# Paddings between the ring of weights and the blocks of h in place of one strip, in a decoder layer of attention and gated linear attention

## The chip, the cores and the metric

The kernel runs on one core of a Trainium2 chip. The metric is the device time of one execution in microseconds (us). Three runs of the kernel before gave a median of 979.86 us (979.69 to 980.12).

## The reference, cut to what matters

One layer for 1024 tokens of width 1024, in float32:

```python
h = rms_norm(x, pre_g)
z = einsum('bsd,de->bse', h, w_in)          # w_in: 1024 x 7184
qa, ka, va, ga, qb, kb, vb, gb, gk_low = split_columns(z)
oa = diff_attention(qa, ka, va, lam)        # 8 heads, two softmax maps each
ob = gla_chunked(qb, kb, vb, log_a)         # 4 heads, from gk_low
y = einsum('bse,ed->bsd', concatenate([oa * silu(ga), ob * silu(gb)]), w_out)
return x + rms_norm(y, post_g)
```

(The norms of `oa` and `ob` are left out here.) The part that the change touches is the first product, `h @ w_in`.

## The kernel before

**Arithmetic.** TensorE multiplies in the type `float32r`, which keeps fewer digits than float32. So each operand is split into a `hi` and a `lo` tile, and a product is three matmuls: hi by hi, lo by hi and hi by lo.

**Stage 1, `h @ w_in`, to about 625 us.** h transposed is cut into four blocks of 512 by 512, and the weights likewise; a pair of column groups (list `pairs`) is computed by seven block products in place of eight (numbers 1 to 7; dictionary `LEFT`, line 319, says which block of h or which sum of blocks each takes: h11, h12, h22, s1 to s4). The list `order` holds all products in the order in which they are done; `go` (line 595) steps through it, prepares the weights of the present and the next three products (`prepare`, `make_weights`), and calls `step`, which calls `multiply` (line 322). A *narrow* product is 12 matmuls: the weights (128 by 128) are the stationary operand and a 512-column row block of h is the moving one. A *wide* product (the values, VA and VB) is 24 matmuls with the roles exchanged: 128 columns of h are stationary and 256 columns of the weights are moving. Results x, y and z stay in banks of PSUM, are copied out by ScalarE (`snap`, line 427) and added by VectorE (line 440).

**Weights.** SyncE loads raw weights to `w_raw`. VectorE forms sums of blocks there (line 296), ScalarE rounds to the hi tile (line 315), VectorE subtracts to the lo tile (line 316). Hi and lo go to the **ring**: five tiles of 4096 bytes in each partition (`tag="ring"`, `bufs=NRING`). A narrow product takes one ring tile for both, a wide pair takes two. Each of the ring's 196 tiles replaces an earlier one: where several are waited for, the pool takes the one that is released first (28 times the tile taken was handed out four before, and 28 times six before; else five).

**Blocks of h.** Each block has hi and lo, each in two pieces of 4096 bytes (s3 and s4 in one piece of 8192). They lie in the pools `hw` and `hpool` at the right end of SBUF. Ahead of `hw` the kernel allocates a strip `edge` of 120 float32 (480 bytes in a partition) at the very end (lines 124 and 125), which nothing reads. When h is no longer needed, the same places of `hw` hold `wo_hi`, `wo_lo` (the weights w_out) and `m_hi`, `m_lo` (the concatenated heads).

**Stage 2, attention and output.** From about 275 us parts of the gated linear attention (`gla`, whose norm is the two matmuls `gms` with the constant `ones` as stationary operand, lines 839 to 841) are strewn into stage 1; `low_rank` (matmuls `gkl_ps`, with `wl2` stationary, 64 columns) and `decay` (`gk`) run early. From about 625 us `merge` interleaves the attention's scores (`sc`), transposes (`wtr`), weighted values (`po`) and the first part of the output product (`ypart`); the rest of that (`yps`) ends the kernel.

**Order.** All matmuls and transposes go through the helpers `mm` (line 117) and `tr` (line 120), which pin them in the program's order, so nearly all TensorE work has line 117. The other engines' instructions are ordered by the recording layer's planner.

**Offsets.** What follows calls the byte address of an operand in its partition, modulo 512, its *offset*. In the program before, all five ring tiles, all blocks of h, `wo`, `m`, q, k, v and the transposed attention weights have offset 0, and since matmul operands begin at multiples of 128 elements in them, so has nearly every matmul operand. The exceptions: `ident` (the moving operand of the transposes) is at 160, `ones` at 192, and `wl2`, whose slices of 64 columns lie alternately at 0 and 256. While one matmul streams its moving operand, the stationary operand of the next is loaded; the *distance* of such a pair is the offset of the operand that is loaded minus that of the one that is streamed, modulo 512.

Of the kernel before, what the change touches and what calls it, by code (L numbers as in the profile page):

```python
# [8 lines left out]
F32 = mybir.dt.float32  # L9
F32R = mybir.dt.float32r  # L10
# [4 lines left out]
P = 128  # L15
# [4 lines left out]
HB = 4  # L20
# [11 lines left out]
def hymba_kernel(  # L32
# [21 lines left out]
    act, dve, pool, pe, sp = nc.scalar, nc.vector, nc.gpsimd, nc.tensor, nc.sync  # L54

    def fp(t):
        return t.bitcast(F32)
# [63 lines left out]

    edge = ctx.enter_context(tc.tile_pool(name="edge", bufs=1, side="right"))
    pool.memset(edge.tile([P, 120], F32, name="edge"), 0.0)
    hw = ctx.enter_context(tc.tile_pool(name="hw", bufs=1, side="right", reuse_waits="tile"))
    hpool_cm = tc.tile_pool(name="hpool", bufs=1, side="right")
    hpool = hpool_cm.__enter__()

    H = {}  # L130

    def block(n):
        if n not in H:
            pool_h, pieces = (hpool, 1) if n in ("s3", "s4") else (hw, 2)
            H[n] = [
                [
                    pool_h.tile(
                        [P, HB // pieces, 512], F32R, tag=f"{n}_{part}{i}", name=f"{n}_{part}"
                    )
                    for i in range(pieces)  # L140
                ]
                for part in ("hi", "lo")
            ]
        return H[n]
# [5 lines left out]
    for n in ("h11", "h12"):  # L150
        block(n)
# [3 lines left out]
    ap = ap_cm.__enter__()  # L155
# [25 lines left out]
    def wide(p):  # L181
        return pairs[p][0] in ("VA", "VB")
# [3 lines left out]
    def load_raw(p, halves=(0, 1)):  # L186
        if p >= len(pairs):
            return
        c0 = pairs[p][2]
        for kh in halves:  # L190
            if kh not in raws.setdefault(p, {}):
                r = ap.tile([P, HB, 256], F32, tag="raw", name="w_raw", bufs=4)
                rows = slice(kh * 512, kh * 512 + 512)
                sp.dma_start(r, w_in[0, rows, c0 : c0 + 256].rearrange("(k p) c -> p k c", p=P))
                raws[p][kh] = r
# [21 lines left out]
    i = order.index((1, 4))  # L217
# [20 lines left out]
    def prepare(i):  # L238

        if i >= len(order) or i in ws:  # L240
            return
        if i < 4:

            act_ins, dve_ins = normed[0][:2]
            with tc.issue_after(act_ins.ins), tc.issue_after(dve_ins.ins):
                make_weights(i)
        else:
            make_weights(i)

    def fetch_raw(p, n, i):  # L250

        if not wide(p):
            load_raw(p)
            if i >= n_early:
                load_raw(p + 1)
        elif p >= 4 or p == 0:
            load_raw(p)
            if p and n == 1:
                load_raw(p + 1)

            if n == 4:
                load_raw(p + 2, (0,))
                if p == 0:
                    load_raw(3, (0,))
            elif n == 7:
                if p == 0:
                    load_raw(3, (1,))
                else:
                    load_raw(p + 2, (1,))
        else:  # L270
            if n == 5:
                load_raw(2, (1,))
            elif n == 4:
                load_raw(4, (0,))
            elif n == 7:
                load_raw(4, (1,))

    def make_weights(i):
        p, n = order[i]
        if wide(p) and p % 2:  # L280
            ws[i] = ws_wide[p - 1, n]
            return
        if p in early and n < 3:
            src = early[p][n - 1]
        else:
            fetch_raw(p, n, i)
            if wide(p):
                (b11, b21), (b12, b22) = ([raws[q].get(kh) for kh in range(2)] for q in (p, p + 1))
            else:
                top, bot = raws[p][0], raws[p][1]  # L290
                b11, b12 = top[:, :, :P], top[:, :, P:]
                b21, b22 = bot[:, :, :P], bot[:, :, P:]


            def sub(dst, a, b):
                dve.tensor_tensor(dst, a, b, ALU.subtract)  # L296
                return dst

            if n == 5:
                src = sub(b11, b12, b11)  # L300
            elif n == 6:
                src = sub(b11, b22, b11)
            elif n == 4:
                src = sub(b21, b21, b11)
            elif n == 7:
                src = sub(b12, b22, b12)
            else:
                src = {1: b11, 2: b21, 3: b22}[n]
        if wide(p):
            w = [ap.tile([P, HB, 256], F32R, tag="ring", name="w", bufs=NRING) for _ in range(2)]  # L310
            ws_wide[p, n] = w
        else:
            w2 = ap.tile([P, 2, HB, P], F32R, tag="ring", name="w", bufs=NRING)
            w = [w2[:, 0], w2[:, 1]]
        act.copy(w[0], src)  # L315
        dve.tensor_tensor(w[1], src, fp(w[0]), ALU.subtract)  # L316
        ws[i] = w

    LEFT = {1: "h11", 2: "h12", 3: "s4", 4: "h22", 5: "s1", 6: "s2", 7: "s3"}
    NRING = 5  # L320
# [224 lines left out]
    def parts(n, j, f):  # L545
        hi, lo = block(n)
        act.copy(at(hi, j), f)
        dve.tensor_tensor(at(lo, j), f, fp(at(hi, j)), ALU.subtract)  # L548

    def blocks(j):  # L550


        pss = []
        for k in (j, j + HB):
            ps, i = take_bank([P, 512], "xT")
            for n in range(4):
                tr(ps[:, n * P : (n + 1) * P], xs[4 + n][:, k * P : (k + 1) * P])
            pss.append(ps)
            free.append(i)
        k = j + HB  # L560
        h21 = t_c("h21")
        act.activation(h21, pss[0], AF.Copy, scale=pre_g[:, j : j + 1])
        put(pss[1], k, block("h22"), j)
        s1 = t_c("s1")
        dve.scalar_tensor_tensor(s1, pss[1], pre_g[:, k : k + 1], h21, ALU.mult, ALU.add)
        parts("s1", j, s1)
        h11 = f1[0][:, j]
        dve.tensor_tensor(h21, h11, h21, ALU.subtract)
        dve.tensor_tensor(h11, s1, h11, ALU.subtract)
        parts("s2", j, h11)  # L570
        parts("s3", j, h21)
# [436 lines left out]
    w, used, scored, opened = {}, set(), [], {}  # L1008
# [517 lines left out]
```

## Time and profile before

| | |
|---|---|
| median of 3 runs | 979.86 us |
| profiled execution | 979.08 us, of which the profile's span is 977.4 us |
| granted TensorE clock, mean | 0.999 |
| VectorE, ScalarE, GpSimd busy | 735.4, 600.5, 142.9 us |
| moved by DMA | 220.45 MB, mean 226 GB/s |

How to read it: the page has the busy time of each engine (PE is TensorE's matmuls, PEld its weight loads, DVE VectorE, ACT ScalarE, POOL GpSimd), then the span in 40 slices, then the chain of work that ended last. A matmul's recorded duration covers its way through the array and overlaps with the next one's. So the rate of TensorE is read from the *starts*: in the timeline a row has the start of a run of equal matmuls and ends in their count (x8), and the next row's start less this one's, divided by the count, is the time per matmul.

### The profile page before, as it was taken

The page shows a single profiled execution, that of the slowest core. Times are in us where ns is not written, and L with a number is a line of the kernel's source. Part 1 is how long each engine was busy: PE and PEld are TensorE (multiplying, and loading weights), DVE is VectorE, ACT ScalarE, POOL GpSimd, SP SyncE. Part 2 cuts the span into 40 slices and gives each one's busy share as a digit, 9 for nine tenths or more (in the row PEclk, how much of TensorE's full clock was granted, in tenths as well). Part 3 has the DMA queues.
Part 4 walks back from the last instruction along what each step waited for, and adds up shares of the span by engine and source line. Part 5 has one row for each costly group of instructions (what it writes and reads, how often), then busy time and mean ns, then how long its engine had stood idle before and what let it go on. Part 6 is the DMA issues. An engine that isn't in the chain of part 4 may idle for free.

```text
span 977.4 us, 15766 instructions
## 1 busy us (share of the span) xinstructions
PE 956.7 (98%) x5338; PEld 830.4 (85%) x5338; DVE 735.4 (75%) x1452; ACT 600.5 (61%) x1164; POOL 142.9 (15%) x158
## 2 busy tenths in 40 slices
PE   5999999999999999999999999999999999999997
PEld 5998988888889998999888888878888888888785
DVE  6887597789866667686786876487888888898554
ACT  8742455487357455454665775366776687887773
POOL 4300000000000010000200002121322222443321
PEclk9999999999999999999999999999999999999999
DMA  9432446656774868897987866987656669994677
GB/s 345 151 110 91 139 135 205 231 179 225 238 247 162 264 187 286 254 294 229 293 259 243 273 202 191 407 269 272 197 186 228 240 199 344 340 294 105 151 208 147
DMA packets 152593, 220.45 MB, mean 226 GB/s; under 512 B 17104, under 2 KB 83664, under 8 KB 152416
## 3 DMA queue, kind: packets, MB, share of 16 engines
q1 hardware_dynamic: 146176, 203.71, 64.1%
q0 software_dynamic: 6336, 15.73, 7.0%
q8 instruction: 42, 0.69, 0.3%
q14 instruction: 39, 0.32, 0.1%
HBM read 133.93 MB, written 88.60 MB: 228 GB/s over the span
## 4 chain that ended last, share of the span: by engine, by line
PE 95%; DVE 2%; ACT 1%; DMA 1%; issue 1%; POOL 0%; SPq 0%; DVEq 0%; ACTq 0%; POOLq 0%
PE x L117 24%; PE y L117 15%; PE z L117 15%; PE ypart L117 13%; PE sc L117 7%; PE po L117 5%; PE yps L117 4%; PE wtr L120 3%; PE gpo L117 3%; PE kv L117 1%; PE gkl_ps L117 1%; PE pa L117 1%; DMA x<-in_x_dram 1%; PE xT L120 1%; DVE s_lo L548 0%
## 5 line engine op out<-in xcount | busy, mean ns | idle before, releaser
L315 ACT CAST w<-w_raw 128x512 fp32r<-128x512 f32 (+1 forms) x164 | 112.4, 688 | 94.7 <-PE y L117 44.1
L316 DVE TENSOR_TENSOR w<-w_raw,w 128x512 fp32r<-128x512 f32 (+1 forms) x164 | 126.7, 774 | 50.1 <-ACT w L315 43.3
L1049 ACT ACTIVATE p<-p,stt 128x896 f32<-128x896 f32 (+7 forms) x128 | 99.3, 777 | 36.7 <-DVE stt L1039 33.9
L427 ACT COPY s<-x 128x512 f32<-128x512 f32 x84 | 49.1, 585 | 84.4 <-PE x L117 84.3
L775 POOL TENSOR_SCALAR_AFFINE_SELECT gan<-gan 128x512 f32<-128x512 f32 x8 | 16.5, 2060 | 485.4 <-ACT gan L774 449.8
L296 DVE TENSOR_TENSOR w_raw<-w_raw 128x512 f32<-128x512 f32 (+1 forms) x96 | 75.9, 791 | 13.9 <-DMA w_raw<-in_w_in_dram 12.6
L1039 DVE CUSTOM_DVE_ANT_0 p<-sc,maskt 128x512 f32<-128x512 f32 (+3 forms) x128 | 74.3, 585 | 14.5 <-PE sc L117 13.3
L117 PE MATMUL ypart<-wo_hi,m_hi 128*128 128x512 f32 x192 | 79.5, 414 | 0.1
L117 PE MATMUL y<-h_hi,w 128*128 128x512 f32 x320 | 79.6, 391 | 0.0
L117 PE MATMUL z<-s_hi,w 128*128 128x512 f32 x320 | 79.6, 391 | 0.0
L117 PE MATMUL x<-s_hi,w 128*128 128x512 f32 x320 | 79.6, 391 | 0.0
L1055 POOL TENSOR_SCALAR p<-p,stt,lam 128x1024 f32<-128x1024 f32 (+3 forms) x64 | 56.2, 879 | 146.9 <-DVE stt L1054 141.9
L117 PE MATMUL ypart<-wo_hi,m_lo 128*128 128x512 f32 x192 | 75.5, 393 | 0.0
L117 PE MATMUL ypart<-wo_lo,m_hi 128*128 128x512 f32 x192 | 75.4, 393 | 0.0
L117 PE MATMUL sc<-k,q 128*128 128x512 f32 (+1 forms) x192 | 69.0, 363 | 1.3 <-DVE stt L1039 1.2
L117 PEld LDWEIGHTS x<-s_hi,w 128*128 128x128 f32 x320 | 59.7, 188 | 12.2
L117 PEld LDWEIGHTS y<-h_hi,w 128*128 128x128 f32 x320 | 59.6, 188 | 12.2
L117 PEld LDWEIGHTS z<-s_hi,w 128*128 128x128 f32 x320 | 59.5, 188 | 12.0
L117 PE MATMUL sc<-ks,q 128*128 128x512 f32 (+1 forms) x192 | 66.1, 347 | 0.0
L1097 ACT CAST wt_hi<-wtr 128x512 fp32r<-128x512 f32 (+1 forms) x80 | 42.7, 534 | 24.6 <-PE wtr L120 23.8
L1098 DVE TENSOR_TENSOR wt_lo<-wtr,wt_hi 128x512 fp32r<-128x512 f32 (+1 forms) x80 | 50.7, 633 | 8.6 <-ACT wt_hi L1097 8.0
L1058 DVE SCALAR_TENSOR_TENSOR p<-p,stt,p 128x1024 f32<-128x1024 f32 (+3 forms) x64 | 52.1, 814 | 4.1 <-POOL p L1055 3.9
(226 smaller groups left out, 2247.7 us busy)
## 6 DMA issues: line engine op xcount, KB each, us to landing
w_raw<-in_w_in_dram SPq DMA_DIRECT2D x56, 512.0 KB, 4.7
wo_raw<-in_w_out_dram SPq DMA_DIRECT2D x32, 256.0 KB, 3.0
wo_d<-wo_hi SPq DMA_DIRECT2D x32, 256.0 KB, 2.8
wo_d<-wo_raw SPq DMA_DIRECT2D x32, 256.0 KB, 3.8
q<-q_d SPq DMA_DIRECT2D x32, 256.0 KB, 4.7
k<-k_d SPq DMA_DIRECT2D x32, 256.0 KB, 5.7
ks<-k_d SPq DMA_DIRECT2D x64, 128.0 KB, 6.2
v<-v_d SPq DMA_DIRECT2D x16, 512.0 KB, 7.0
```

The costliest lines, as they stand in the source:

```text
L117: tc.keep_in_program_order(pe.matmul(*a, **k))
L120: tc.keep_in_program_order(pe.transpose(dst, src, ident))
L296: dve.tensor_tensor(dst, a, b, ALU.subtract)
L315: act.copy(w[0], src)
L316: dve.tensor_tensor(w[1], src, fp(w[0]), ALU.subtract)
L427: act.copy(b[k], ps)
L1039: ins = dve.tensor_tensor_reduce(p[:, a:e], sc[:, : e - a], maskt[:, NZ + P - (e - a) :] if last else maskt[:, : e - a], 1.0, 3e38 if i == ...
L1049: act.activation(p[:, :n], p[:, :n], AF.Exp, bias=st[:, m : m + 1], scale=-1.0, accum_out=st[:, 2 + m : 3 + m],)
L1055: pool.tensor_scalar(p1[:, :n], p1[:, :n], st[:, 5:6], lam, ALU.mult, ALU.mult)
L1058: dve.scalar_tensor_tensor(p0[:, :n], p0[:, :n], st[:, 4:5], p1[:, :n], ALU.mult, ALU.subtract)
L1097: act.copy(hi[:, :n], pt[:, :n])
L1098: dve.tensor_tensor(lo[:, :n], pt[:, :n], fp(hi[:, :n]), ALU.subtract)
```

## The change

The strip goes. Paddings take its 480 bytes: 8, 8, 16, 32 and 0 float32 behind the five ring tiles (256 bytes), and 8, 8, 16 and 24 behind the four pieces of h11 (224 bytes). The ring's tiles get a tag each and are handed out strictly in turn.

```diff
-    edge = ctx.enter_context(tc.tile_pool(name="edge", bufs=1, side="right"))
-    pool.memset(edge.tile([P, 120], F32, name="edge"), 0.0)
...
+    PAD = {"h11_hi0": 8, "h11_hi1": 8, "h11_lo0": 16, "h11_lo1": 24}
+
+    def half(pool_h, k, name, i):
+        t = pool_h.tile([P, k * 512 + PAD.get(f"{name}{i}", 0)], F32R, tag=f"{name}{i}", name=name)
+        return t[:, : k * 512].rearrange("p (k c) -> p k c", c=512)
...
-                [
-                    pool_h.tile(
-                        [P, HB // pieces, 512], F32R, tag=f"{n}_{part}{i}", name=f"{n}_{part}"
-                    )
-                    for i in range(pieces)
-                ]
+                [half(pool_h, HB // pieces, f"{n}_{part}", i) for i in range(pieces)]
...
+    n_ring = [0]
+
+    def ring_tile():
+        i = n_ring[0] % NRING
+        n_ring[0] += 1
+        t = ap.tile([P, 1024 + (8, 8, 16, 32, 0)[i]], F32R, tag=f"ring{i}", name="w")
+        return t[:, :1024]
...
-            w = [ap.tile([P, HB, 256], F32R, tag="ring", name="w", bufs=NRING) for _ in range(2)]
+            w = [ring_tile().rearrange("p (k c) -> p k c", c=256) for _ in range(2)]
             ws_wide[p, n] = w
         else:
-            w2 = ap.tile([P, 2, HB, P], F32R, tag="ring", name="w", bufs=NRING)
+            w2 = ring_tile().rearrange("p (i k c) -> p i k c", i=2, c=P)
```

The offsets of the two built programs:

| tiles | before | after |
|---|---|---|
| the five ring tiles | 0 | 0, 32, 64, 128, 256 |
| h11: hi, hi, lo, lo | 0 | 256, 288, 320, 384 |
| h12, h22, s1, s2 (later wo, m) | 0 | 480 |
| s3, s4, and the scores p0 in their place | 0 | 256 more than before |
| tiles s, c, st, gu, wo_raw behind the ring | 0 | 256 |
| q, k, v, the transposed weights, `w_raw`, x of the last four blocks | 0 | 0 |

The matmuls and transposes stand in the same order in both programs. Some instructions of VectorE, ScalarE and SyncE in stage 1 change places with a neighbour, and one GpSimd memset (the strip's) is gone.

## The prediction

> **What bounds the kernel now.** I read the page first, then what TensorE waits for, then its starts in the timeline.
>
> ```profile
> PE 956.7 (98%) x5338; PEld 830.4 (85%) x5338; DVE 735.4 (75%) x1452; ACT 600.5 (61%) x1164; POOL 142.9 (15%) x158
> ...
> PEclk9999999999999999999999999999999999999999
> ...
> PE 95%; DVE 2%; ACT 1%; DMA 1%; issue 1%; POOL 0%; SPq 0%; DVEq 0%; ACTq 0%; POOLq 0%
> ```
> ```profile
> PE xT L120 <- DVE x L482: 9.4, 4, 7.2
> ```
> ```profile
> 100.00:277.00 177.00, 177.00 (x856) 149.71 (x855) 143.45 (x232) 98.25 (x166) 0.00 (x0) 1.00 0.61 196
> 277.00:600.00 323.00, 323.00 (x1968) 289.41 (x1967) 232.48 (x357) 188.93 (x332) 16.48 (x8) 1.00 0.76 241
> ```
>
> The reader is to see that TensorE is the chain (95%), at full clock, and that its longest wait, 9.4 us in all, is the one at the start, for the normed x. From 100 to 600 us it is busy in the whole of each window. So nothing but the time per matmul can move that half of the kernel, and a faster VectorE, ScalarE or DMA is worth nothing there. The question is whether an operand's place in SBUF changes the time per matmul, and so I read that from the starts.
>
> ```profile
> 135.49 0.61 PE L117 MATMUL gk<-gkl,ku 128*128 128x512 f32 x2
> 135.94 1.98 PE L117 MATMUL z<-s_hi,w 128*128 128x512 f32 x8
> 137.75 1.07 PE L117 MATMUL z<-s_lo,w 128*128 128x512 f32 x4
> 138.66 1.98 PE L117 MATMUL z<-s_hi,w 128*128 128x512 f32 x8
> ```
> ```profile
> 126.00:278.00 152.00, 152.00 (x672) 125.88 (x671) 127.34 (x211) 87.64 (x150) 0.00 (x0) 1.00 0.65 212
> ```
>
> One narrow product, 12 matmuls, takes 138.66 - 135.94 = 2.72 us: 226.7 ns each; the eight of its first row take 1.81 us, 226 each. The window of 152 us touches 672, of which it cuts those at its edges: 152 us are 670.6 times 226.7 ns, so the rhythm holds over 56 products, whatever VectorE and ScalarE did meanwhile. I call this the locked rhythm. All operands there have offset 0. The two `gk`, of other tiles but at offset 0 too, do not disturb it: the eight behind them take 1.81 us.
>
> Now the only places in the trace where full-width matmuls have another distance than 0. In `gms` the stationary `ones` is at 192; in `gkl_ps` every second stationary operand is at 256.
>
> ```profile
> 384.61 0.62 PE L117 MATMUL gms<-sq_hl,ones 128*128 128x512 f32 x2
> 385.07 2.00 PE L117 MATMUL y<-h_hi,w 128*128 128x512 f32 x8
> 386.91 0.84 PE L117 MATMUL y<-h_lo,w 128*128 128x512 f32 x3
> ```
> ```profile
> 76.72 2.00 PE L117 MATMUL gkl_ps<-h_hi,wl 128*64 128x512 f32 x8
> 78.56 2.00 PE L117 MATMUL gkl_ps<-h_lo,wl 128*64 128x512 f32 x8
> 80.39 0.28 PE L117 MATMUL z<-w,s_hi 128*128 128x256 f32 x1
> ```
>
> After two `gms` the eight of y take 386.91 - 385.07 = 1.84 us, 230.0 ns each. That is 3.3 more than 226.7, though they are at distance 0 again themselves. The first eight `gkl_ps` take 1.84 us, 230.0 each, the next 1.83, 228.8 each. Sixteen in a row don't find the locked rhythm again. It isn't offset alone that disturbs: in the attention stage, all at 0 but for `ident`, the shapes change every few matmuls, and
>
> ```profile
> 706.56 0.40 PE L117 MATMUL ypart<-wo_hi,m_hi 128*128 128x512 f32 x1
> ...
> 708.39 0.28 PE L117 MATMUL sc<-k,q 128*128 128x256 f32 x1
> ```
>
> has eight full-width matmuls between these two starts in 1.83 us, 228.8 each.
>
> **The change part by part.**
>
> *Narrow products.* The rows of the narrow products are eight, from
>
> ```profile
> L117 PE MATMUL y<-h_hi,w 128*128 128x512 f32 x320 | 79.6, 391 | 0.0
> ...
> L117 PE MATMUL x<-h_lo,w 128*128 128x512 f32 x80 | 21.4, 389 | 0.0
> ```
>
> with counts of 3 x 320 + 4 x 160 + 80 = 1680 matmuls. By the addresses of the two built programs nearly all of them have distance 0 before; after, 109 keep it and 1571 don't (32 to 480 bytes, mostly 32, 64, 96, 160 and 288, since most blocks of h are at 480 and the ring at 0 to 256). No row shows a long run at one distance other than 0. Bounds: at worst the whole loss after `gms` is the price of its two matmuls: 384.61 to 386.91 is 2.30 us for ten, 2.27 at 226.7, so 0.033 us or 16 ns each, +25 us. At best, equal offsets are themselves a collision, and the part of a matmul that doesn't grow with its columns goes:
>
> ```profile
> 118.83 2.08 PE L117 MATMUL z<-w,s_hi 128*128 128x256 f32 x16
> 120.74 1.12 PE L117 MATMUL z<-w,s_lo 128*128 128x256 f32 x8
> 121.70 2.08 PE L117 MATMUL z<-w,s_hi 128*128 128x256 f32 x16
> ```
>
> 24 matmuls of 256 columns take 2.87 us by these starts (2.88 below), 120 each; 512 cost 106.7 more, so 256 columns cost 106.7 and 13.3 ns are fixed: -13.3 x 1571 = -21 us. I take +3.3 ns, the 230.0 of `gkl_ps` and behind `gms`, the nearest rows: 1571 x 3.3 = **+5.2 us**.
>
> *Wide products.* They too lose distance 0 (1344 matmuls of 256 columns). But here a disturbed rhythm costs nothing: the product behind another pair of `gms`
>
> ```profile
> 309.54 2.08 PE L117 MATMUL x<-w,h_hi 128*128 128x256 f32 x16
> 311.46 1.13 PE L117 MATMUL x<-w,h_lo 128*128 128x256 f32 x8
> 312.42 2.08 PE L117 MATMUL x<-w,h_hi 128*128 128x256 f32 x16
> ```
>
> takes 312.42 - 309.54 = 2.88 us for 24, 120.0 each, as the undisturbed one. **0**; at most 3.3 x 1344 = 4.4 us, at best a gain of the same size.
>
> *Output product and attention.* The tail is locked now,
>
> ```profile
> 959.81 10.89 PE yps L117 x48
> ```
>
> 226.9 ns each. After, 97 of its 193 matmuls have distance 32: 97 x 3.3 = **+0.3 us**. Of the 918 full-width `ypart`, `sc` and `po` 402 get a distance, but their rhythm is broken already (228.8): 402 x (230.0 - 228.8) = **+0.5 us**, between -5 (402 x 13.3) and +6 (402 x 16).
>
> *The other engines.* Their operands move too, but durations don't show places:
>
> ```profile
> L315 ACT CAST w<-w_raw x164: 601/622/1058, 11.6 to 617.3; 128x512 fp32r<-128x512 f32 x138, 128x1024 fp32r<-128x1024 f32 x26
> L316 DVE TENSOR_TENSOR w<-w_raw,w x164: 671/689/1630, 12.7 to 617.9; 128x512 fp32r<-128x512 f32 x138, 128x1024 fp32r<-128x1024 f32 x26
> ```
>
> From least to median is 3% although TensorE, the other engine and DMAs ran beside them at every phase (the maxima are the wide form). And TensorE's work covers them: if each of the 138 casts took those 21 ns more, it would be 2.9 us in stage 1, all hidden. **0**.
>
> *Ring strictly in turn.* In 28 wide cases the lo tile, free after two thirds of its last product, was taken first; now the hi tile, free at its end, is waited for: a third of 2.88 us = 0.96 us later. ScalarE's cast, and behind it in its queue the copies from PSUM, wait that much longer:
>
> ```profile
> ACT w L315 <- PE y L117: 44.1, 24, 5.5
> ...
> PEld x L117 <- DVE w L316: 0.3, 1, 0.3
> ```
>
> ScalarE waits 44.1 us for such releases already, and TensorE's loads waited for a weight once, 0.3 us: weights are made three products (over 8 us) ahead. **0**; if all were exposed, 28 x 0.96 = 27 us; the same rows give no gain above 0.3.
>
> *The strip's memset* (GpSimd, at 2 us, before x arrives) goes: **0**, since TensorE starts only when VectorE has normed x.
>
> Sum: 5.2 + 0.3 + 0.5 = +6.0 on the profiled 979.08 (span 977.4 and 1.7 around it): 985.1. The median of the runs is 0.8 above the profiled one: **985.9 us**.
>
> **Rivals.**
>
> *Place doesn't matter* (chance 0.23). What I see behind `gms` would come from something else (the same stationary operand twice), and in `gkl_ps` from 64 columns; for it speaks that wide-to-narrow changes at offset 0 break the rhythm as well. Then all terms are 0: 979.9 us. The Trainium skill says so: "TensorE: Matmul & The Clock Gate", Part 2, gives TensorE two independent read ports and says that loading the next weights takes no bandwidth from the running matmul, and "SBUF — State Buffer", section "Who interferes with whom", says that PE and ACT never wait on anyone. By that rule the sum is 0; the 672 matmuls at 226.7 agree, the 230.0 of `gkl_ps` does not obviously.
>
> *Equal offsets collide* (0.17; the other side: faster). At distance 0 the load and the stream begin in the same place, and a share of the fixed 13.3 ns is that collision. Full price 21 us: 959; half: 969. It decides from 1.3 ns per matmul on (1571 x 1.3 = 2 us). Against it: the fixed part is the same at 256 and 512 columns, and no row with a distance is below 226.7.
>
> *Distances cost more than a lost rhythm* (0.12): each load collides in mid-stream. Half of the 16 ns bound is 1571 x 8 = 12.6: 993; the whole, 1005.
>
> *A stall of the ring* (0.03): a tenth of the 27 us: 982.6.
>
> **How the numbers follow.** The lost rhythm has 0.45. 0.2% is 2 us, about what a measurement of this kernel can tell from no change. Slower by more: 0.45 + 0.12 + 0.03 = 0.60; same 0.23; faster 0.17. The range leaves out most of the faster case (0.14) and the dearer half of the collisions (0.06): 976 to 995.
>
> **What would show it.** Right: narrow products in the windows 126 to 278 us at about 2.76 us per 12 in place of 2.72, and the wide ones still at 2.88; no new waits of PE. Wrong: 2.72 again (place doesn't matter), less than 2.72 (equal offsets collided), or a PE wait for `w` in the list of waits (the ring). Stage 1 should end some 5 us later, and the rest keep its length within 1 us.

## The result and the profile after

The changed kernel takes 986.22 us (median of 4 runs, 985.57 to 987.60); the kernel before, on the same chip, 979.99 (979.69 to 980.48). The ratio is 1.0065, with a 95% interval of 1.0048 to 1.0082: 6.2 us slower. The profiled execution took 985.91 us, with a span of 984.2 (6.8 more than before).

The page of after, and its list of TensorE's waits:

```profile
PE 963.8 (98%) x5338; PEld 827.4 (84%) x5338; DVE 734.1 (75%) x1452; ACT 601.6 (61%) x1164; POOL 145.2 (15%) x157
...
PEclk9999999999999999999999999999999999999999
...
PE 86%; DVE 5%; ACT 3%; DMA 3%; issue 1%; SPq 1%; POOL 0%; DVEq 0%; ACTq 0%
```
```profile
PE xT L120 <- DVE x L489: 9.0, 4, 7.3
...
PE gms L117 <- DVE sq_hl L842: 0.2, 1, 0.2
```

TensorE's busy time grew by 7.1 us with the same 5338 instructions at the same clock. Its waits are those of before, also in the rows left out (each within 0.1 us), but for two rows: the one for the normed x, 9.4 us before and 9.0 now, and the last, 0.2 us, which is new. The chain's 86% in place of 95% isn't idle TensorE, which is busy for 98% of the span as before: where several things end together the chain follows one of them, here more often another engine's. So the 6.8 us are in the matmuls themselves. The stretch of narrow products, by windows (PE's matmuls come first, with their count), and its starts in the timeline:

```profile
126.00:278.00 152.00, 152.00 (x656) 123.00 (x655) 123.94 (x203) 87.52 (x150) 0.00 (x0) 1.00 0.64 208
```
```profile
119.88 2.07 PE L117 MATMUL z<-w,s_hi 128*128 128x256 f32 x16
...
122.74 2.03 PE L117 MATMUL y<-h_hi,w 128*128 128x512 f32 x8
...
137.19 2.03 PE L117 MATMUL z<-s_hi,w 128*128 128x512 f32 x8
139.06 1.10 PE L117 MATMUL z<-s_lo,w 128*128 128x512 f32 x4
140.00 2.03 PE L117 MATMUL x<-s_hi,w 128*128 128x512 f32 x8
...
145.60 1.98 PE L117 MATMUL x<-s_hi,w 128*128 128x512 f32 x8
147.42 1.08 PE L117 MATMUL x<-s_lo,w 128*128 128x512 f32 x4
148.33 2.02 PE L117 MATMUL x<-h_hi,w 128*128 128x512 f32 x8
```

The same 152 us touch 656 matmuls, not 672. The narrow product at 137.19, whose operands are at distance 96, takes 140.00 - 137.19 = 2.81 us (2.72 before); its first eight take 1.87 us, 234 ns each. Not all of them do: the one at 145.60, at distance 256, takes 1.82 for eight and 2.73 in all, as before. A wide product takes 122.74 - 119.88 = 2.86 us (2.87 and 2.88 before). The end is the output product; in the chain of before and of after it is one unbroken run:

```profile
936.42 34.28 PE yps L117 x151
```
```profile
942.64 34.90 PE yps L117 x151
```

It went from 227.0 to 231.1 ns each. Adding up start to start over all matmuls of a kind, in both profiled executions (sums over the whole trace, with each matmul's addresses from the built program), gives:

| | before, us | after, us | difference |
|---|---|---|---|
| narrow products, 1680 matmuls | 382.9 | 391.4 | +8.5 |
| wide products, 1344 | 166.2 | 163.2 | -2.9 |
| `yps`, 193 | 44.6 | 45.2 | +0.6 |
| `ypart`, `sc`, `po` | 266.2 | 266.6 | +0.4 |
| `xT`, `gms`, `gkl_ps` together | 24.6 | 24.7 | +0.1 |

That is the 6.8 us of the span, to 0.1. Two terms make the result, of opposite sign. Sorted by distance (within products, without the gaps that waits make), the narrow matmuls of after take 228.3 to 228.5 ns at 0 and 256, about 229 at 192, and 230 to 234 at all others; the wide ones lie between 116 and 119.5, against 119.8 before.

### The profile page after: what moved, and what is told of

It is laid out like the page before. It is cut to its first block, busy times and chain, and to the rows that moved or that the text cites. A ratio compares the mean times of both kernels' runs of the same rounds, so it can differ in the third digit from the quotient of the medians.

```text
span 984.2 us, 15763 instructions
## 1 busy us (share of the span) xinstructions
PE 963.8 (98%) x5338; PEld 827.4 (84%) x5338; DVE 734.1 (75%) x1452; ACT 601.6 (61%) x1164; POOL 145.2 (15%) x157
## 4 chain that ended last, share of the span: by engine, by line
PE 86%; DVE 5%; ACT 3%; DMA 3%; issue 1%; SPq 1%; POOL 0%; DVEq 0%; ACTq 0%
PE x L117 21%; PE z L117 13%; PE ypart L117 13%; PE y L117 13%; PE sc L117 7%; PE po L117 5%; PE yps L117 4%; PE wtr L120 3%; PE gpo L117 2%; DMA wo_raw<-in_w_out_dram 1%; PE kv L117 1%; PE gkl_ps L117 1%; DVE w L323 1%; DMA k_d<-qk_st 1%; DMA v_d<-c 1%
## 5 line engine op out<-in xcount | busy, mean ns | idle before, releaser
L782 POOL TENSOR_SCALAR_AFFINE_SELECT gan<-gan 128x512 f32<-128x512 f32 x8 | 19.2, 2404 | 487.1 <-ACT gan L781 487.1
L117 PEld LDWEIGHTS z<-s_hi,w 128*128 128x128 f32 x320 | 59.5, 188 | 13.3
```

Of the source, the lines that this page charges most:

```text
L117: tc.keep_in_program_order(pe.matmul(*a, **k))
```

## The experiments

**D**: the distance sets the time of a matmul. **O**: the ring's new order, or what the planner makes of it, does it. **A**: operands must start at multiples of 512 bytes, whatever the other's place. Beside them stands the rival of the prediction, place doesn't matter. Ratios are to the kernel before on the same chip, with 95% intervals; times per matmul are means over the trace, start to start, of the matmuls within a product. They leave out the few long gaps at waits and at the beginnings of products, which the sums of the table above hold: before, 227.1 ns narrow and 119.8 wide without them, 227.9 and about 124 with them.

**1. The ring in turn, without paddings** (after, with the strip kept)

```diff
+    edge = ctx.enter_context(tc.tile_pool(name="edge", bufs=1, side="right"))
+    pool.memset(edge.tile([P, 120], F32, name="edge"), 0.0)
-    PAD = {"h11_hi0": 8, "h11_hi1": 8, "h11_lo0": 16, "h11_lo1": 24}
+    PAD = {}
-        t = ap.tile([P, 1024 + (8, 8, 16, 32, 0)[i]], F32R, tag=f"ring{i}", name="w")
+        t = ap.tile([P, 1024], F32R, tag=f"ring{i}", name="w")
```

> The changed kernel's tags and its strict turn of the ring's tiles, but no paddings, and the strip back: all offsets 0 again. Theory D (the distance between the operand that is loaded and the one that is streamed sets the time per matmul): 980.0 us, within 0.7, narrow products at 226.7 ns a matmul, wide ones at 120. Theory O (the order of the ring and the planner's new order cost it): 986, with waits of PE or of its loads.

Measured: 979.20 us, ratio 0.9994 (0.9984 to 1.0005). Timeline:

```profile
134.71 1.98 PE L117 MATMUL z<-s_hi,w 128*128 128x512 f32 x8
...
137.43 1.98 PE L117 MATMUL z<-s_hi,w 128*128 128x512 f32 x8
```

Narrow products take 137.43 - 134.71 = 2.72 us again. The total is 0.8 us below the 980.0 that D gave, just outside its 0.7, and level with before. O falls: order, tags and planner together cost nothing. The engines' instructions stand here in the same order as in after, but for the strip's memset.

**2. Only the strip goes** (before without it, no padding: h lies at 480 as a whole, the ring at 0; narrow distance 32, wide 480)

```diff
-    edge = ctx.enter_context(tc.tile_pool(name="edge", bufs=1, side="right"))
-    pool.memset(edge.tile([P, 120], F32, name="edge"), 0.0)
```

> The kernel before without the strip and with no padding: all blocks of h at offset 480, the ring at 0, so narrow products have the one distance 32 and wide ones the one distance 480. By the changed kernel's rows for these distances (233.2 ns narrow against 227.1, 117.8 wide against 119.9, 233.3 for half of the tail) theory D gives 1680 x 6.1 = +10.2, 1344 x -2.1 = -2.8 and 97 x 6 = +0.6, so 988 us (985 to 990). If a spread of several offsets were what costs, and not a distance as such, it would be 980.

Measured: 986.80 us, ratio 1.0067 (1.0053 to 1.0081). The window and the timeline:

```profile
126.00:278.00 152.00, 152.00 (x653) 122.38 (x652) 123.69 (x202) 87.17 (x149) 0.00 (x0) 1.00 0.64 206
```
```profile
119.84 2.03 PE L117 MATMUL z<-w,s_hi 128*128 128x256 f32 x16
...
122.64 2.03 PE L117 MATMUL y<-h_hi,w 128*128 128x512 f32 x8
...
125.43 2.03 PE L117 MATMUL x<-s_hi,w 128*128 128x512 f32 x8
```

Two lines less, and the whole loss is there, with every engine's instructions in the order of before but for the strip's memset: narrow 2.79 us per 12, wide 2.80 per 24. Over the trace that is 233.3 ns in place of 227.1, and 116.9 in place of 119.8. One distance, held throughout, costs as much as the spread; so "place doesn't matter" falls. The output product has both kinds side by side: 226.95 ns at distance 0, 233.27 at 32.

**3. All at 128** (a constant of 128 bytes ahead of the ring and all that follows it, the strip shortened by as much: ring, h, q, k, v, wo and m at offset 128, the distances among them as before; `ident` and `ones` stay where they were)

```diff
+    shift = const.tile([P, 32], F32, name="shift")
+    pool.memset(shift, 0.0)
...
-    pool.memset(edge.tile([P, 120], F32, name="edge"), 0.0)
+    pool.memset(edge.tile([P, 88], F32, name="edge"), 0.0)
```

> The kernel before with one unused tile of 128 bytes among the constants and a strip of 352: ring, h, q, k, v, wo, m all at offset 128, so the distances are 0 as before, but nothing begins at a multiple of 512 bytes. Theory D: 980.0 us, within 0.7, 226.7 ns narrow. Theory A (an operand that doesn't begin at a multiple of 512 bytes costs more by itself): narrow products near 233 ns, 988 us or more.

Measured: 980.30 us, ratio 1.0000 (0.9988 to 1.0012). Timeline (with two lines more ahead of it, the helper `mm` is at line 119):

```profile
134.66 1.98 PE L119 MATMUL z<-s_hi,w 128*128 128x512 f32 x8
...
137.38 1.98 PE L119 MATMUL z<-s_hi,w 128*128 128x512 f32 x8
```

2.72 us. A falls: it is the difference of the two places that counts.

**4. `ident` and `ones` at 0** (before, with the small constants allocated ahead of them; each distance within the kernel's main matmuls is 0; shown are the first lines that move)

```diff
+    eps_t = const.tile([P, 1], F32, name="eps_t")
+    dsteps = [const.tile([P, NT], F32, name=f"dstep{g}") for g in range(GLA_HEADS)]
...
     ident = const.tile([P, P], F32, name="ident")
+    ones = const.tile([P, P], F32R, name="ones")
```

> The kernel before with its small constants allocated ahead of ident and ones, which so come to offset 0: every pair of load and stream in the program has distance 0. Theory D: the eight matmuls behind gms take 1.81 us in place of 1.84, and the transposes of the attention no longer have distance 352; gms alone is worth 8 x 0.03 = 0.2 us, the transposes from 0 to some 2 us: 978 to 980. If the broken rhythm behind gms comes from loading the same operand twice, 1.84 stays, and 980.0.

Measured: 979.51 us, ratio 0.9996 (0.9987 to 1.0005). Timeline, behind a pair of `gms` (`mm` is at line 120 here):

```profile
383.55 0.62 PE L120 MATMUL gms<-sq_hl,ones 128*128 128x512 f32 x2
384.00 1.98 PE L120 MATMUL y<-h_hi,w 128*128 128x512 f32 x8
385.82 1.07 PE L120 MATMUL y<-h_lo,w 128*128 128x512 f32 x4
```

The eight behind `gms` now take 1.82 us, not 1.84. In all four places of the trace where a narrow product follows `gms`, the eight take 1.81 us by the unrounded starts, and 1.83 before. So it was the distance 192 of `ones` that disturbed them, and not that `ones` is loaded twice. The transposes take 108.9 ns at distance 0 as they did at 352, so distance makes no difference to them. The attention stays about as it was too (`ypart` 230.4, 230.9 before), with all its operands at distance 0: there something else, which wasn't looked into, keeps the matmuls above 227. (`gkl_ps` keeps its distances 0 and 256 here, so not every pair of the program is at 0.)

**5. to 8. One distance at a time** (before, with another length of the strip: h moves, the ring stays at 0, and all instructions keep their order; 56 puts h at 256, 104 at 64, 88 at 128 and 72 at 192)

```diff
-    pool.memset(edge.tile([P, 120], F32, name="edge"), 0.0)
+    pool.memset(edge.tile([P, 56], F32, name="edge"), 0.0)
```

> The kernel before with a strip of 224 bytes in place of 480: h at 256, the ring at 0, the distance 256 throughout the products. In the changed kernel's trace pairs at 256 keep the rhythm (228.3 ns narrow, 119.1 wide), so theory D with a period of 256 bytes: 979.5 us, 978.5 to 981. With a period of 512 (256 as bad as the rest, 233): 988.

> As before, strip of 416: h at 64; narrow at distance 448. That is 192 in a period of 256, where the changed kernel has twelve pairs at 229.1 ns alone; wide at 64, not there at all. With 229 narrow: 1680 x 2 = +3.4, wide between 0 and -5: 978 to 983. If 192 is as bad as the others (233): +10 and 985 to 990.

> As before, strip of 352: h at 128; narrow at distance 384 (232.1 ns in the changed kernel), wide at 128 (118.3). Theory D: 1680 x 5.0 = +8.4, 1344 x -1.5 = -2.0, tail +0.5: 986.9 us.

> As before, strip of 288: h at 192; narrow at distance 320 (232.4 ns in the changed kernel), wide at 192 (116.1, the lowest there). Theory D: 1680 x 5.3 = +8.9, 1344 x -3.8 = -5.1, tail +0.5: 984.3 us. If narrow depended on the distance's sign only through period 256 (64: 233.3): 985.8.

| h at | narrow distance: ns | wide distance: ns | us | ratio |
|---|---|---|---|---|
| 0 (before) | 0: 227.1 | 0: 119.8 | | |
| 480 (experiment 2) | 32: 233.3 | 480: 116.9 | 986.80 | 1.0067 |
| 256 | 256: 227.1 | 256: 119.8 | 979.09 | 1.0001 (0.9991 to 1.0010) |
| 64 | 448: 228.9 | 64: 115.1 | 979.18 | 0.9995 (0.9985 to 1.0005) |
| 128 | 384: 233.0 | 128: 119.0 | 989.53 | 1.0094 (1.0079 to 1.0110) |
| 192 | 320: 233.4 | 192: 117.8 | 987.87 | 1.0080 (1.0066 to 1.0094) |

256 is as good as 0, for both kinds. At 64, 128 and 192 the two kinds can be seen to move apart. In the timeline the wide product is the stretch from the first row to the second, the first narrow one that from the second to the third, and the next narrow one that from the third to the fourth; first h at 256, then h at 64, then h at 128:

```profile
120.40 2.08 PE L117 MATMUL z<-w,s_hi 128*128 128x256 f32 x16
...
123.28 2.00 PE L117 MATMUL y<-h_hi,w 128*128 128x512 f32 x8
...
126.03 1.98 PE L117 MATMUL x<-s_hi,w 128*128 128x512 f32 x8
...
128.75 1.98 PE L117 MATMUL x<-h_hi,w 128*128 128x512 f32 x8
```
```profile
119.62 1.98 PE L117 MATMUL z<-w,s_hi 128*128 128x256 f32 x16
...
122.34 1.99 PE L117 MATMUL y<-h_hi,w 128*128 128x512 f32 x8
...
125.09 1.99 PE L117 MATMUL x<-s_hi,w 128*128 128x512 f32 x8
...
127.84 1.99 PE L117 MATMUL x<-h_hi,w 128*128 128x512 f32 x8
```
```profile
120.83 2.08 PE L117 MATMUL z<-w,s_hi 128*128 128x256 f32 x16
...
123.71 2.02 PE L117 MATMUL y<-h_hi,w 128*128 128x512 f32 x8
...
126.49 2.02 PE L117 MATMUL x<-s_hi,w 128*128 128x512 f32 x8
...
129.29 2.02 PE L117 MATMUL x<-h_hi,w 128*128 128x512 f32 x8
```

h at 256: wide 2.88 us, narrow 2.75 and 2.72. h at 64: wide 2.72, narrow 2.75 and 2.75. At 128: 2.88, 2.78 and 2.80. The first narrow product behind a wide one takes 2.75 at distance 256 too, so the loss is read from the second. With h at 64 all narrow matmuls lose 3.3 us and the wide ones win 5.2, and the total is within 0.2% of before. The expectations for 128 and 192 were about 3 us too low, from both kinds: the wide products keep less of the gain there than I had taken, 2.0 ns at 192 in place of 3.8 and 0.8 at 128 in place of 1.5, and the narrow ones lose about 1 ns more.

**9. to 11. Wide at 64, 32 and 96, narrow at 0** (if wide products gain at 64 and narrow ones lose, give each its own distance: experiment 1 with one contiguous ring, h at 64, narrow weights 64 bytes into the place in the ring, wide ones at its start; the second and third with 32 and 96. In the code `at` is 0 for wide and 16 for narrow products)

```diff
-    pool.memset(edge.tile([P, 120], F32, name="edge"), 0.0)
+    pool.memset(edge.tile([P, 104], F32, name="edge"), 0.0)
...
+    ring = ap.tile([P, NRING * 1024 + 16], F32R, tag="ring", name="w")
...
+        return ring[:, i * 1024 + at : i * 1024 + at + 1024]
```

Here the last 64 (32, 96) bytes of a narrow place are also the first of the next, and a wide place there overwrites them, so part of those products is computed with other weights.

> One contiguous ring in strict turn; narrow weights 64 bytes behind the place of wide ones, h at 64 (strip of 416): narrow products keep distance 0, wide ones get 64, which was their fastest so far (115.1 ns a matmul against 119.8). Theory D, each pair of load and stream on its own: 1344 x -4.8 = -6.4, the tail's half at 448 +0.2: 973.8 us (972.5 to 975.5), faster than both kernels. If what the wide products gain is lost again where wide and narrow ones follow each other: 976 to 980.

> The same with 32 bytes in place of 64 (h at 32): narrow at 0, wide at 32, for which the changed kernel has eight pairs alone (118.4 ns). Theory D: 1344 x -1.4 = -1.9: 978 us.

> The same with 96 bytes (h at 96): wide at 96, between 64 (115.1 ns) and 128 (119.0): some 117, 1344 x -2.8 = -3.8: 976 us.

Measured: 1024.68, 1028.26 and 1027.85 us; ratios 1.0455 (1.0439 to 1.0471), 1.0491 (1.0473 to 1.0508) and 1.0482 (1.0449 to 1.0515). All three missed their expectations by some 50 us, but the times per matmul are near those that D gives: narrow 227.2 to 227.3, wide 115.3 at 64, 118.4 at 32, and 118.0 at 96, where 117 was guessed. What is new is that TensorE's matmuls wait for weights, for which they waited no more than 0.6 us in any run outside these three. The first (64), its waits and two of its windows:

```profile
PE x L117 <- DVE w L327: 19.7, 9, 6.0
PE z L117 <- DVE w L327: 13.8, 4, 5.6
...
PE y L117 <- DVE w L327: 4.4, 4, 2.0
```
```profile
20.00:126.00 106.00, 82.03 (x582) 76.25 (x580) 67.10 (x102) 38.15 (x60) 9.85 (x10) 0.92 0.34 104
126.00:278.00 152.00, 150.43 (x743) 127.51 (x744) 119.98 (x196) 86.32 (x146) 0.00 (x0) 1.00 0.58 181
```

37.9 us of waits; in the 106 us from 20 to 126 TensorE is busy for 82 and its granted clock is 0.92 (in this window of before it is 1.00). All five places are views of one tile that overlap, so the write to a place also waits for readers of its neighbour; that this is the cause of the waits fits with the next run, where only that is mended, but it wasn't tried by itself. Added up start to start, the wide products with their waits take 202.1 us in place of 166.2, and the transposes of x with theirs 19.7 in place of 13.6: 42 of the 44 us. These three measure the distances and are no candidates.

**12. The same with a tile for each place** (experiment 1 with longer ring tiles, no overlaps; the room comes from a fourth buffer of `st`, which goes; `at` as in 9)

```diff
-        return t2k("st", 4, name, dt)
+        return t2k("st", 3, name, dt)
...
-    pool.memset(edge.tile([P, 120], F32, name="edge"), 0.0)
+    pool.memset(edge.tile([P, 360], F32, name="edge"), 0.0)
...
+        t = ap.tile([P, (1088, 1088, 1088, 1088, 1040)[i]], F32R, tag=f"ring{i}", name="w")
+        return t[:, at : at + 1024]
```

> The same distances as in the contiguous ring (narrow 0 or 256, wide 64 or 320), but five tiles of their own: four of 4352 bytes and one of 4160, wide weights at their beginning, narrow ones 64 bytes behind; room from three st buffers in place of four, strip of 1440, so h at 64. Theory D with period 256: wide at 115.1 to 115.3 ns, narrow at 227.1: 1344 x -4.7 = -6.3, tail +0.2: 973.9 us (972.5 to 976), faster than both kernels. If three st buffers hold up ScalarE so that TensorE waits: 976 or more, with PE waits for s or w.

Measured: 977.23 us (975.23 to 978.48, 6 runs) beside 980.74; ratio 0.9960 (0.9948 to 0.9972): faster than both kernels, by 3.5 us against before. Timeline and waits:

```profile
119.16 2.05 PE L117 MATMUL z<-w,s_hi 128*128 128x256 f32 x16
...
121.99 1.98 PE L117 MATMUL y<-h_hi,w 128*128 128x512 f32 x8
...
124.71 1.98 PE L117 MATMUL x<-s_hi,w 128*128 128x512 f32 x8
```
```profile
PE gpo L117 <- DVE gu L812: 1.8, 1, 1.8
...
PE gms L117 <- DVE sq_hl L844: 0.9, 1, 0.9
```

Narrow 2.72 us, wide 2.83 in this product; over the trace 227.2 and 115.9. The wide products gain 5.1 us (166.2 to 161.1) and the narrow ones lose 0.5. I had expected 973.9 (972.5 to 976). In this trace about 3 us come back as two waits that before didn't have; `gpo` takes 28.2 us in place of 26.1 and `gms` 5.0 in place of 3.7. The trace is of the longest of the six executions (978.48 us), so the others may wait less. The missing `st` buffer is a suspect, but it wasn't tried alone, and it can't be all: experiments 1 to 8 keep all four buffers and show the wait of `gpo` for `gu` too, with 0.2 to 1.3 us.

## Why the prediction came out

**Total and direction.** 985.9 was forecast, 986.2 measured, and the cause is the one forecast: narrow products lose time when the distance is no longer 0. But the total is this near by luck: two errors of the sum, +3.3 us in the narrow products and -2.9 in the wide ones, nearly cancel.

**Narrow products: mis-sized.** The step "I take +3.3 ns, the 230.0 of `gkl_ps` and behind `gms`, the nearest rows" gave +5.2 us; measured +8.5. Neither row was a steady run at a bad distance. (They weren't the only places either: `ones` is also loaded for the matmuls `ms` of the attention and for two `yps`.) The distances in `gkl_ps` are 0 and 256, and 256 is harmless (h at 256: 227.1); its 230.0 must have another reason, perhaps its 64 columns, which wasn't tried. The eight behind `gms` are at distance 0 and only recover from two matmuls at 192 (experiment 4). A steady run costs 6.2 ns (experiment 2). The count was off the other way: of the 1571, 157 are at 256 and nearly keep the rhythm. 8.5 us over the other 1414 are 6.0 ns each, which agrees with it. This lies between the 3.3 ns of the lost rhythm and the 8 ns of the rival "Distances cost more than a lost rhythm", so the total doesn't decide between the two pictures. The starts speak against a rhythm that is merely lost: at distance 32 and 160 they show another regular one (in experiment 2's output product 231 or 232 and 235 ns in turn, in a product of after at 160 twice 231, then 238).

**Wide products: wrong sign.** Forecast 0, and "the wide ones still at 2.88"; measured -2.9 us, 2.2 ns each. That a disturbed rhythm costs nothing there was right, but the 120.0 ns of distance 0 isn't a floor. The rival "equal offsets collide" was given to all products; what it forecasts, less time at any other distance but 256, is seen for the wide ones alone. The reason held against it, that the fixed 13.3 ns is the same at 256 and 512 columns, was weak: it is one number fitted to two, all at distance 0. At distance 64 4.7 ns go for 256 columns, and for 512 columns 6 are added.

**Output product and attention.** +0.6 against +0.3 (97 matmuls at 6.3 ns, not 3.3), and +0.4 against +0.5.

**Other engines, ring in turn, memset: 0.** Right. Experiment 1 has the new order and after has all the new places, and neither shows a new wait for weights.

**Landmarks.** The first `ypart` behind the last product of stage 1, in the timelines of before and of after:

```profile
630.63 0.39 PE L117 MATMUL ypart<-wo_hi,m_hi 128*128 128x512 f32 x1
```
```profile
636.42 0.39 PE L117 MATMUL ypart<-wo_hi,m_hi 128*128 128x512 f32 x1
```

5.8 us later, where "some 5 us" was said; the remaining 1.0 of the 6.8 comes behind it, as said. The narrow product was to take about 2.76 us: the one shown takes 2.81, and not all are alike.

**"Place doesn't matter" and its rule.** The Trainium skill, "TensorE: Matmul & The Clock Gate", Part 2, gives TensorE two independent read ports, by which loading the next weights takes no read bandwidth from the running matmul. Experiment 2 differs from before in places and the strip's memset alone, and its narrow matmuls take 233.3 ns in place of 227.1. Here the measurement decides: the load's place relative to the stream's matters, by 2.7% at 512 columns and up to 4% (119.8 to 115.1) at 256.

## What to carry to other kernels

Where TensorE is the chain and each matmul loads new weights, look at the address of the operand that is loaded less that of the one that is streamed, modulo 256, and choose it per shape: in this kernel 0 for 512 moving columns and 64 bytes for 256. Here the longer ring tiles took 1088 bytes more in each partition, and room taken from a buffer elsewhere may give part of the gain back as waits. To price such an effect take a long run at one place; a row behind a single disturbance shows a recovery, not the steady cost, and changing the length of one strip gives such a run with a single line.

## What was not expected of the hardware

- The time of a matmul depends on the distance and not on the offsets themselves (all at 128: 227.1 and 119.8 ns), and it repeats after 256 bytes: 0 and 256 are alike, narrow matmuls take 233.3 at 64 (in after) and 233.4 at 320, and experiment 12 has wide ones at 64 and 320 with 116.0 and 115.8.
- The dependence differs by shape: with 512 columns 227.1 at 0, 228.9 at 448, 233 at 32, 320 and 384; with 256 columns 119.8 at 0, 118.4 at 32, 115.1 at 64, 118.0 at 96, 119.0 at 128, 117.8 at 192, 116.9 at 480.
- It has a sign: for 512 columns 448 (64 behind) costs 1.8 ns, and 64 ahead costs 6 (233.3, from the 163 such pairs in after).
- Open: what collides. It is the load of the next operand that counts: in the output product of experiment 2 three matmuls in the middle of an even run are at distance 0 from their own stationary operand, while the next one is loaded at distance 32 or 224, and each of these three takes 235 ns, where the three ahead of it take 226 or 227. But no run shows the reads themselves. Distances finer than 32 bytes, other shapes, and the ring's paddings without those of h were not tried.
